# Earlier mark for the first w_up loads, raw pairs in one tile, and w_down's operands in other buffers

## The chip, the cores and the metric

The kernel runs on one core of one Trainium2 chip. The time is the device time of one execution in microseconds (us): a median of runs, and beside it one execution that the hardware profiler took, on which every span and duration below rests. Engines: PE (TensorE), ACT (ScalarE), DVE (VectorE), POOL (GpSimd) and SP (SyncE, which here only issues DMAs). Each engine works through its own instructions in the order of the program; a wait of one instruction holds all that stand behind it on the same engine.

## The reference

Two layers over 512 tokens of 1024 channels, and a last RMSNorm. Of a layer, this is what matters here:

```
mixed = sigmoid(gate_a) * y_a + sigmoid(gate_b) * y_b     # y_b = attention out @ w_o_nsa
x = x + mixed @ w_out                                     # 1024 x 1024
h = rmsnorm(x, norm_mlp)
x = x + square(relu(h @ w_up)) @ w_down                   # 1024 x 4096, 4096 x 1024
```

## The kernel before

**Products.** All is float32. A factor is split in a high part (a cast to fp32r) and a rest, and a product is three matmuls, high x high, high x rest, rest x high. For weights `fetch` (L202) loads a raw block of 512 KB through SP into one of two `raw` buffers, `convert` casts it on ACT (L218, `wh`) and subtracts on DVE (L219, `wl`); `gemm` issues the matmuls, L244 and L245 with `wh` and L246 with `wl`. It converts the next block while one is multiplied. A tile of w_out is 8 steps of three matmuls, 128 x 128 by 128 x 512.

**The end of a layer's attention.** For m = 0..7 the output projection w_o_nsa gives a tile of y_b; L1073 and L1074 (DVE) gate it and add it to MA, four tiles "va" of two halves each: MA[m // 2][:, m % 2]. `mix` (L1055, L1056) halves and splits what is in MA. Then x is loaded, and the loop over w_out's eight tiles runs: `gemm`, L1094 adds the result to x[m], `prepare` scales x[m] and splits it for the MLP (bs L1428, ts L1431, casts L1420 and L1423 on ACT, rests L1421 and L1424 on DVE), `sumsq` squares it on ACT (L288) and adds up on POOL (L298) for the first ones.

**The MLP** is done by a Strassen-like scheme (7 products in place of 8). A unit g takes a pair of w_up's column blocks: `load(g)` loads r2 and r1 (512 KB each, L1476) and s3 (256 KB, L1486) through SP, and POOL issues two DMAs that add within SBUF: r2[:512] += r2[512:] (L1478, the sum s1) and s3 += r1[:512] (L1487). `convert(g)` splits r1 (ACT L1506, DVE L1507), forms a11 = s1 + a11 (DVE L1513), splits r2, forms a12 = a11 + a12 (L1516), splits r1 again and s3. The products of it are the matmuls of L1526. Pairs 0 to 15 are w_up's; 16 to 19 are w_down's last 1024 rows, done the same way in `down` at the MLP's end (L1252 to L1264).

**What sets the order around the change.** The loads of pairs 0 and 1 and the first half of `convert(0)` are issued ahead of and within the w_out loop; unit g loads pair g + 2. To hold the first two pairs' loads back until the attention is over, POOL copies one column of `b.mark` into each of their raw tiles (L1469), and the loads wait for that copy, since they overwrite it:

```
self.mark = MA[3][:, 1, :1]
S.load(0)
S.load(1)
conv = S.convert(0)
```

Buffers are tiles by tag; a tile waits for the last readers of the buffer it takes, and the tiles of the MLP's tags lie over those of the attention. "f" has four buffers of 4 KB a partition (two pairs), "h" two for s3. w_down's Winograd operands b1 and b22 take a "vn", three "q2" and an "hl" tile, and the raw blocks of pairs 18 and 19 the same tags. The scheduler that puts the instructions of each engine in order goes by these buffers, too.

Of the kernel before, what the change touches and what calls it, by code (L numbers as in the profile page):

```python
# [12 lines left out]
F32R = mybir.dt.float32r  # L13
# [130 lines left out]
class Body:  # L144
    def __init__(self, ctx, tc, nc, a):
# [4 lines left out]
        self.ps = P("ps", 2, space=bass.MemoryType.PSUM)  # L150
        self.dp = P("dp", 1, space=bass.MemoryType.DRAM)

    BUFS = dict(raw=2, wh=2, wl=2, u2=8, o2=8, va=4, t2=12, kd=2, kk=1, zz=4, zzm=2, pt=10, long=2, q2=3, vn=1, e=2, cp=2, a4=1, f=4, h=2, a5=2, tmp=3,
                hl=2, r=1, crs=1, zc=4, tt=1, tf=1, small=1, cc=1, s4=6, big=1, g4=2)

    TINY = dict(s4=(4, 12), sm=(4, 8), g4=(4, 2), s16=(16, 2), s32=(32, 5), z=(32, 1), th=(96, 1), gates=(96, 1))
# [1 line left out]
    def t(self, tag, shape, dt=F32, name=None):  # L158
# [8 lines left out]
        if tag in ("tmp", "small") and n < T:  # L167
            v = self.sb.tile([128, T], dt, name=name or tag, tag=tag, bufs=self.BUFS[tag])[:, :n]
            if len(shape) > 2:
# [3 lines left out]
            return v  # L173
        bufs = self.BUFS[tag]
        if tag in self.LOCAL:
            bufs = self.BUFS.get(tag + self.part[0], bufs)
            tag += self.part
# [443 lines left out]
    def compress(self, kc, vc, small, l):  # L621
# [20 lines left out]
        def load(c):  # L642
            for i, raw in enumerate(self.two("o2", "w1", F32) if c < 8 else ()):
                nc.sync.dma_start(raw, a["w1"][l, i, c].rearrange("p j m -> p (j m)"))
                loaded.append(raw)

        load(0)
        load(1)
        for c in range(0, 8, 2):
            load(c + 2)  # L650
            yield
            load(c + 3)
            yield
            w = [loaded.popleft() for _ in range(4)]
            for j in range(4):
                jj = 2 * c + j
                for i in range(2):
                    nc.tensor.matmul(hp[64 * i:64 * i + 64, :256], A[i][jj // 8][:, jj % 8],
                                     w[j // 2 * 2 + i][:, j % 2 * 256:(j % 2 + 1) * 256],
                                     start=jj == 0, stop=jj == 15)  # L660
            yield
            yield
# [97 lines left out]

    BUFS.update(s16=2, sm=8)

# [56 lines left out]

    BUFS.update(th=1, s32=5, gates=1, z=1)  # L820

# [40 lines left out]
    def layer(self, l, u):  # L862
        nc, a = self.nc, self.a
# [3 lines left out]
        va = [self.p(t) for t in ("S", "S", "PT", "PT")]  # L867
# [3 lines left out]
        g = self.token_proj(src, 512, va, u)  # L871
# [7 lines left out]
        g = self.token_proj([[a["wg2"][l, c].rearrange("p j m -> p (j m)")] for c in range(4)], 288, g2, u)  # L879
# [18 lines left out]
        for b in range(NB):  # L898
            pv = g2[b][:, :256].rearrange("p (h d) -> p h d", h=4)
            r = rc[:, b:b + 1]  # L900
# [14 lines left out]
        st, hl = {}, []  # L915
# [59 lines left out]
        MA = [self.t("va", [128, 2, T], name="ma") for _ in range(4)]  # L975
# [83 lines left out]
        for m in range(8):  # L1059
# [12 lines left out]
            t, y = st["gb", m], MA[m // 2][:, m % 2]  # L1072
# [9 lines left out]
            nc.scalar.dma_start(x[k], self.x_src[k])  # L1082
        self.part = f"m{l}"
        S = Strassen(self, l, x, self.gain[:, 16 * l + 8:16 * l + 16])
        self.mark = MA[3][:, 1, :1]
        S.load(0)
        S.load(1)
        conv = S.convert(0)
# [118 lines left out]
class Strassen:  # L1207
# [190 lines left out]
    def prepare(self, m):  # L1398

        b, nc = self.b, self.nc  # L1400
        V, A = nc.vector, nc.scalar
        f = lambda ap: ap.bitcast(F32)
        if m == 0:
            k12 = [b.t("kd", [128, 2, 2, 2, 256], F32R, name="t12") for _ in range(2)]
            k34 = [b.t("long", [128, 2, 2, 2, 256], F32R, name="t34") for _ in range(2)]
            self.k12 = [t[:, i] for t in k12 for i in range(2)]
            self.k34 = [t[:, i] for t in k34 for i in range(2)]
            t = b.t("vn", [128, 2, 2, 2, 256], F32R, name="b1")
            self.k1 = [t[:, 0], t[:, 1]] + [b.t("q2", [128, 2, 2, 256], F32R, name="b1") for _ in range(2)]
            k22 = [b.t(tag, [128, 2, 2, 256], F32R, name="b22") for tag in ("q2", "hl")]  # L1410
            self.k22 = [t[:, i] for t in k22 for i in range(2)]
            t1, t2 = ([t[:, i] for t in self.k12] for i in range(2))
            t3, t4 = ([t[:, i] for t in self.k34] for i in range(2))
            n11, b21 = ([t[:, i] for t in self.k1] for i in range(2))
            self.xs = dict(a11=n11, s1=t1, s2=t2, a22=t4, s3=t3, a12=b21, s4=self.k22)
            self.b1 = {}

        def split(o, x, sign=1.0):
            if sign == 1.0:
                A.copy(o[..., 0, :], x)  # L1420
                V.tensor_tensor(o[..., 1, :], x, f(o[..., 0, :]), op=OP.subtract)  # L1421
            else:
                A.activation(o[..., 0, :], x, AF.Copy, scale=sign)  # L1423
                V.scalar_tensor_tensor(o[..., 1, :], x, sign, f(o[..., 0, :]), op0=OP.mult, op1=OP.subtract)  # L1424

        p = m % 4
        t = b.t("t2", [128, T], name="bs")
        A.activation(t, self.x[m], AF.Copy, scale=self.gm[:, m:m + 1])  # L1428
        if m < 4:
            d = b.t("t2", [128, 2, 256], name="ts")  # L1430
            V.tensor_tensor(d[:, 0], t[:, 256:], t[:, :256], op=OP.subtract)  # L1431
            split(self.k1[p][:, 0], t[:, :256], -1.0)
            split(self.k12[p][:, 0], d[:, 0])
            self.b1[p] = t, d
            return
        t1, d = self.b1.pop(p)
        split(self.k1[p][:, 1], t[:, :256])
        V.tensor_tensor(d[:, 1], t[:, 256:], d[:, 0], op=OP.subtract)
        split(self.k12[p][:, 1], d[:, 1])
        t34 = b.t("t2", [128, 2, 256], name="ts")  # L1440
        V.tensor_tensor(t34[:, 1], t[:, :256], d[:, 1], op=OP.subtract)
        V.tensor_tensor(t34[:, 0], t1[:, 256:], t[:, 256:], op=OP.subtract)
        split(self.k34[p], t34)
        split(self.k22[p], t[:, 256:], -1.0)
# [5 lines left out]
    def load(self, g, third=True):  # L1450

        b = self.b
        if g == 18:
            r = b.t("vn", [128, 2, 1024], name="raw")
            self.rest = [b.t("q2", [128, 2, 512], name="raw") for _ in range(3)]

            for t in [r] + self.rest[1:]:
                self.nc.scalar.copy(t[:, :, :1], self.c[3][:, :, :1])
            r2, r1 = r[:, 0], r[:, 1]
            s3 = self.rest[0][:, 0]  # L1460
        elif g == 19:
            r2, r1 = (t.rearrange("p a c -> p (a c)") for t in self.rest[1:])
            s3 = self.rest[0][:, 1]
        else:
            r2, r1 = (b.t("f", [128, 1024], name="raw") for _ in range(2))
            s3 = b.t("h", [128, 512], name="raw")
            if g < 2:
                for t in (r2, r1, s3):
                    self.nc.gpsimd.tensor_copy(t[:, :1], b.mark)  # L1469
        r1, r2, s3 = self.raw[g] = r1[:, :1024], r2[:, :1024], s3[:, :512]  # L1470
        if g > 17:
            self.nc.sync.dma_start(r1, self.source(g, 1))
            self.nc.sync.dma_start(r2, self.source(g, 0))
            return
        for i, t in enumerate((r2, r1)):
            self.nc.sync.dma_start(t, self.source(g, i))  # L1476
            if t is r2:
                self.nc.gpsimd.dma_start(r2[:, :512], r2[:, 512:], accum_op=OP.add)  # L1478
        if third:
            self.third(g)  # L1480
# [162 lines left out]
```

## Time and profile before

| | us |
|---|---|
| median of 3 runs | 1518.62 (1518.27 to 1518.7) |
| the profiled execution | 1516.23 |
| its span, first to last instruction | 1514.2 |
| DVE busy | 1153.2 |
| ACT busy | 809.8 |

The span is what the profile's times count from; 2 us of the profiled execution lie around it. In a view's row the first number is the start or the busy time, in brackets stands how long the engine idled just before and what it waited for; `x` is the number of instructions. Matmuls overlap in the pipeline: their starts tell the pace, not their lengths. PEclk, or the granted clock, is the share of full speed that PE was given. The mean over the span is 0.995.

The stage of the change in layer 0 runs from about 354 us (the second w_o) to about 422 us (end of w_out), in layer 1 from about 1103 to 1171 us.

### The profile page before, as it was taken

Reading aid. Unit: us, or ns where it says so; the run is one execution under the profiler, and the core shown is the slowest. Engines: PE = TensorE matmul, PEld = TensorE weight load, DVE = VectorE, ACT = ScalarE, POOL = GpSimd, SP = SyncE. Lnnn points to the kernel's source line nnn. Section 1 sums busy time; section 2 is a strip of 40 time slices with the busy share of each in tenths; the row PEclk is TensorE's granted clock in tenths of the full one; section 3 lists DMA queues with packets and bytes.
Section 4 is the critical chain, followed back from the end, with each engine's and each line's share of the span. In section 5 each row is a group of like instructions: output and inputs, shape, how many; then the busy total and the mean of one; then the engine's idle time right before and its main releaser. Section 6 shows DMA issues by size and latency. Waiting matters only on the chain.

```text
span 1514.2 us, 23498 instructions
## 1 busy us (share of the span) xinstructions
PE 1492.2 (99%) x8766; PEld 1299.9 (86%) x8766; DVE 1153.2 (76%) x2245; ACT 809.8 (53%) x1536; POOL 121.2 (8%) x161
## 2 busy tenths in 40 slices
PE   9999999999899999999999999999998999999998
PEld 8888888888699998999988788888876999999998
DVE  5678979777787776678847799787679777677795
ACT  6465656554574444455545556555546544445455
POOL 1010000000300000010010000000013100000112
PEclk9999999999999999999999999999999999999999
DMA  7654422124645555564267552221355555455532
GB/s 249 187 166 126 140 70 70 70 71 155 198 129 148 144 138 146 144 165 110 85 205 186 156 130 92 84 72 69 114 163 148 158 149 137 133 143 139 140 99 70
DMA packets 73921, 200.50 MB, mean 132 GB/s; under 512 B 9264, under 2 KB 10672, under 8 KB 73808
## 3 DMA queue, kind: packets, MB, share of 16 engines
q1 hardware_dynamic: 58256, 171.19, 35.9%
q0 software_dynamic: 11520, 20.98, 8.4%
q10 hardware_dynamic: 4032, 6.84, 1.4%
q8 instruction: 69, 1.13, 0.3%
q14 instruction: 44, 0.36, 0.1%
HBM read 150.67 MB, written 4.19 MB: 102 GB/s over the span
## 4 chain that ended last, share of the span: by engine, by line
PE 75%; issue 19%; DVE 3%; DMA 2%; ACT 0%; POOL 0%; POOLq 0%; SPq 0%; DVEq 0%; ACTq 0%
PE ps_S L1526 8%; PE ps_mm L244 7%; PE ps_mm L245 7%; PE ps_mm L246 7%; PE ps_PT L1526 5%; PE ps_O L244 4%; PE ps_O L246 4%; PE ps_mm L1526 4%; PE ps_O L245 4%; PE ps_O L1526 2%; PE ps_mm L1319 2%; PE ps_S L1319 1%; PE ps_O L612 1%; PE ps_PT L586 1%; PE ps_S L561 1%
## 5 line engine op out<-in xcount | busy, mean ns | idle before, releaser
L218 ACT CAST wh<-raw 128x1024 fp32r<-128x1024 f32 (+2 forms) x161 | 164.7, 1024 | 173.4 <-PE ps_mm L245 51.1
L219 DVE TENSOR_TENSOR wl<-raw,wh 128x1024 fp32r<-128x1024 f32 (+2 forms) x161 | 191.7, 1191 | 33.0 <-ACT wh L218 32.3
L1507 DVE TENSOR_TENSOR s<-raw,s 128x1024 fp32r<-128x1024 f32 (+1 forms) x128 | 139.0, 1087 | 81.9 <-ACT s L1506 81.7
L244 PE MATMUL ps_mm<-u,wh 128*128 128x512 f32 x480 | 192.7, 402 | 0.0
L246 PE MATMUL ps_mm<-u,wl 128*128 128x512 f32 x480 | 189.2, 394 | 0.0
L245 PE MATMUL ps_mm<-u,wh 128*128 128x512 f32 x480 | 189.0, 394 | 0.0
L1506 ACT CAST s<-raw 128x1024 fp32r<-128x1024 f32 (+1 forms) x128 | 120.5, 942 | 80.3 <-PE ps_mm L1526 26.2
L246 PE MATMUL ps_O<-o,wl 128*128 128x512 f32 x280 | 110.2, 393 | 5.8 <-DVE wl L219 5.8
L244 PE MATMUL ps_mm<-o,wh 128*128 128x512 f32 x288 | 113.7, 395 | 0.0
L245 PE MATMUL ps_mm<-o,wh 128*128 128x512 f32 x288 | 113.1, 393 | 0.0
L246 PE MATMUL ps_mm<-o,wl 128*128 128x512 f32 x288 | 112.9, 392 | 0.0
L244 PE MATMUL ps_O<-o,wh 128*128 128x512 f32 x280 | 110.2, 393 | 0.4 <-ACT wh L218 0.4
L245 PE MATMUL ps_O<-o,wh 128*128 128x512 f32 x280 | 110.0, 393 | 0.0
L246 PEld LDWEIGHTS ps_mm<-u,wl 128*128 128x128 f32 x480 | 90.2, 188 | 18.9
L244 PEld LDWEIGHTS ps_mm<-u,wh 128*128 128x128 f32 x480 | 90.5, 189 | 17.9 <-DVE E L462 0.8
L245 PEld LDWEIGHTS ps_mm<-u,wh 128*128 128x128 f32 x480 | 90.4, 188 | 15.7 <-issue 0.4
L1526 PEld LDWEIGHTS ps_S<-t,s 128*128 128x128 f32 x768 | 98.7, 189 | 4.7 <-ACT z L1565 0.4
L1526 PE MATMUL ps_S<-t,s 128*128 128x256 f32 x768 | 101.0, 281 | 0.0
L590 ACT CAST pth<-ps_PT 128x384 fp32r<-128x384 f32 (+1 forms) x96 | 49.0, 513 | 64.8 <-PE ps_PT L586 64.7
L1603 ACT ACTIVATE z<-z 128x512 f32<-128x512 f32 x64 | 40.3, 633 | 78.1 <-DVE z L1602 77.9
L548 DVE CUSTOM_DVE_ANT_0 E<-ps_S,ct 128x384 f32<-128x384 f32 (+3 forms) x112 | 57.2, 513 | 31.7 <-PE ps_S L561 30.8
L549 ACT ACTIVATE E<-E,tiny 128x384 f32<-128x384 f32 (+3 forms) x112 | 65.6, 586 | 20.4 <-DVE tiny L548 20.2
(357 smaller groups left out, 3396.9 us busy)
## 6 DMA issues: line engine op xcount, KB each, us to landing
raw<-wb SPq DMA_DIRECT2D x64, 512.0 KB, 3.2
raw<-wup SPq DMA_DIRECT2D x64, 512.0 KB, 4.3
raw<-wd SPq DMA_DIRECT2D x48, 512.0 KB, 3.7
raw<-raw POOLq DMA_DIRECT2D x80, 256.0 KB, 3.7
w<-w SPq DMA_DIRECT2D x32, 256.0 KB, 4.6
kda<-hla SPq DMA_DIRECT2D x32, 256.0 KB, 4.3
q2a<-hla SPq DMA_DIRECT2D x64, 128.0 KB, 2.3
raw<-wo SPq DMA_DIRECT2D x16, 512.0 KB, 4.4
```

The source lines that it names most:

```text
L218: nc.scalar.copy(h[:, :n], raw[:, :n])
L219: nc.vector.tensor_tensor(lo[:, :n], raw[:, :n], h[:, :n].bitcast(F32), op=OP.subtract)
L244: mm(ps, h[:, c], xh, start=start and i == 0, stop=False)
L245: mm(ps, h[:, c], xl, start=False, stop=False)
L246: mm(ps, lo[:, c], xh, start=False, stop=stop and i == ks - 1)
L548: nc.vector.tensor_tensor_reduce(e, ps, self.mask[:, T - n:], -1.0, BIG, OP.add, OP.min, mx)
L549: nc.scalar.activation(e, e, AF.Exp, bias=mx, scale=-1.0, accum_out=un["sm"][:, i:i + 1])
L590: nc.scalar.copy(h[:, e, :n], ps[:, :n])
L1319: mm = lambda o, *z, **kw: nc.tensor.matmul(o, *z, skip_group_check=True, **kw)
L1506: nc.scalar.copy(h, src)
L1507: nc.vector.tensor_tensor(lo, src, h.bitcast(F32), op=OP.subtract)
L1526: mm = lambda o, *z, **kw: self.nc.tensor.matmul(o, *z, skip_group_check=True, **kw)
```

## The change

The mark becomes MA[0]'s second half, which is the gate's second tile. A pair's r2 and r1 are one tile of 8 KB, with two such buffers in place of four of 4 KB; b1, b22 and the raw blocks of pairs 18 and 19 take "vn" buffers, of which the MLP has three. Behind these lines the new program is four lines shorter, so L1469 is now L1465, L1476 L1472, L1486 L1482, L1506 and L1507 L1502 and L1503, L1513 L1509, L1516 L1512. All of the attention's and MLP's tiles get new addresses: the first two pair tiles now lie side by side at the low end of SBUF, over the attention's keys (tag "kk").

```diff
-... q2=3, vn=1, e=2, cp=2, a4=1, f=4, h=2 ...
+... q2=3, vn=1, vnm=3, e=2, cp=2, a4=1, f=2, h=2 ...
...
-        self.mark = MA[3][:, 1, :1]
+        self.mark = MA[0][:, 1, :1]
...
-            t = b.t("vn", [128, 2, 2, 2, 256], F32R, name="b1")
-            self.k1 = [t[:, 0], t[:, 1]] + [b.t("q2", [128, 2, 2, 256], F32R, name="b1") for _ in range(2)]
-            k22 = [b.t(tag, [128, 2, 2, 256], F32R, name="b22") for tag in ("q2", "hl")]
-            self.k22 = [t[:, i] for t in k22 for i in range(2)]
+            k1 = [b.t("vn", [128, 2, 2, 2, 256], F32R, name="b1") for _ in range(2)]
+            self.k1 = [t[:, i] for t in k1 for i in range(2)]
+            t = b.t("vn", [128, 4, 2, 256], F32R, name="b22")
+            self.k22 = [t[:, i] for i in range(4)]
...
-        if g == 18:
+        if g > 17:
             r = b.t("vn", [128, 2, 1024], name="raw")
-            self.rest = [b.t("q2", [128, 2, 512], name="raw") for _ in range(3)]
-
-            for t in [r] + self.rest[1:]:
-                self.nc.scalar.copy(t[:, :, :1], self.c[3][:, :, :1])
-            r2, r1 = r[:, 0], r[:, 1]
-            s3 = self.rest[0][:, 0]
-        elif g == 19:
-            r2, r1 = (t.rearrange("p a c -> p (a c)") for t in self.rest[1:])
-            s3 = self.rest[0][:, 1]
+            self.nc.scalar.copy(r[:, :, :1], self.c[3][:, :, :1])
+            if g == 18:
+                self.third18 = b.t("vn", [128, 2, 512], name="raw")
+            r2, r1, s3 = r[:, 0], r[:, 1], self.third18[:, g - 18]
         else:
-            r2, r1 = (b.t("f", [128, 1024], name="raw") for _ in range(2))
+            t = b.t("f", [128, 2, 1024], name="raw")
+            r2, r1 = t[:, 0], t[:, 1]
             s3 = b.t("h", [128, 512], name="raw")
```

On SP, behind the four loads of the second w_o in either layer, the difference of the two programs is this (wup are the pairs' loads, r2, r1 and the 512 wide s3; a line with + is the new program's):

```order
+L1472 DMA raw<-wup 128x1024
+L202 DMA raw<-wout 128x1024
+L1472 DMA raw<-wup 128x1024
+L1482 DMA raw<-wup 128x512
+L202 DMA raw<-wout 128x1024
+L1472 DMA raw<-wup 128x1024 x2
+L1482 DMA raw<-wup 128x512
 L202 DMA raw<-wout 128x1024 x3
-L1476 DMA raw<-wup 128x1024 x2
-L1486 DMA raw<-wup 128x512
-L202 DMA raw<-wout 128x1024 x2
```

Pair 0's first load stands ahead of w_out's first, its two others behind that; pair 1's stand behind w_out's second load. Before, all of them stood behind w_out's third.

On DVE, in the w_out loop from x of m = 1 (ps_S is the second tile's bank) the order before is this, with the three rows ahead of it (s is a split of a raw block, 1024 wide for r1 or r2 and 512 for s3; wl in the last row but one is that of m = 3):

```order
L1507 TENSOR_TENSOR s<-raw,s 128x1024
L1421 TENSOR_TENSOR t_3742<-ts,t_3742 128x256
L1507 TENSOR_TENSOR s<-raw,s 128x1024
L1513 TENSOR_TENSOR raw<-raw 128x512
L1094 TENSOR_TENSOR x<-x,ps_S 128x512
L1516 TENSOR_TENSOR raw<-raw 128x512
L1507 TENSOR_TENSOR s<-raw,s 128x512
L1431 TENSOR_TENSOR ts<-bs 128x256
L219 TENSOR_TENSOR wl<-raw,wh 128x1024
L1507 TENSOR_TENSOR s<-raw,s 128x1024
```

And this it is in the new program, to the row behind wl of m = 4:

```order
L1503 TENSOR_TENSOR s<-raw,s 128x1024
L1421 TENSOR_TENSOR t_3740<-ts,t_3740 128x256
L1509 TENSOR_TENSOR raw<-raw 128x512
L1503 TENSOR_TENSOR s<-raw,s 128x512
L1503 TENSOR_TENSOR s<-raw,s 128x1024
L1094 TENSOR_TENSOR x<-x,ps_S 128x512
L1512 TENSOR_TENSOR raw<-raw 128x512
L219 TENSOR_TENSOR wl<-raw,wh 128x1024
L1431 TENSOR_TENSOR ts<-bs 128x256
L1503 TENSOR_TENSOR s<-raw,s 128x1024
L1424 SCALAR_TENSOR_TENSOR b_3744<-bs,b_3744 128x256
L1421 TENSOR_TENSOR t_3740<-ts,t_3740 128x256
```

The splits of s3 and r2 stand ahead of x of m = 1, and wl of m = 3 one row earlier, ahead of ts; behind the last row shown come x of m = 2, one more split (of pair 1's first block), ts, b and then wl of m = 4, which before stood right behind x of m = 2.

On POOL, at the end of layer 0's MLP, the DMAs that add within SBUF stood before in this order (the two pairs are 16 and 17; L1478 is r2's, L1487 s3's, L1264 belongs to `down`):

```order
L1478 DMA raw_6653<-raw_6653 128x512
L1487 DMA raw_6655<-raw_6654 128x512
L1478 DMA raw_6661<-raw_6661 128x512
L1487 DMA raw_6663<-raw_6662 128x512
L1264 DMA raw_6654<-raw_6654 128x512
L1264 DMA raw_6662<-raw_6662 128x512
```

Now they stand so:

```order
L1483 DMA raw_6636<-raw_6635 128x512
L1474 DMA raw_6635<-raw_6635 128x512
L1483 DMA raw_6643<-raw_6642 128x512
L1474 DMA raw_6642<-raw_6642 128x512
L1264 DMA raw_6635<-raw_6635 128x512
L1264 DMA raw_6642<-raw_6642 128x512
```

In either pair s3's sum is now ahead of r2's.

More of the change, by code (lines that the diff above doesn't have):

```diff
@@ L151, in __init__ @@
         self.dp = P("dp", 1, space=bass.MemoryType.DRAM)
-    BUFS = dict(raw=2, wh=2, wl=2, u2=8, o2=8, va=4, t2=12, kd=2, kk=1, zz=4, zzm=2, pt=10, long=2, q2=3, vn=1, e=2, cp=2, a4=1, f=4, h=2, a5=2, tmp=3,
+    BUFS = dict(raw=2, wh=2, wl=2, u2=8, o2=8, va=4, t2=12, kd=2, kk=1, zz=4, zzm=2, pt=10, long=2, q2=3, vn=1, vnm=3, e=2, cp=2, a4=1, f=2, h=2, a5=2, tmp=3,
                 hl=2, r=1, crs=1, zc=4, tt=1, tf=1, small=1, cc=1, s4=6, big=1, g4=2)
```

## The prediction

> **What bounds the kernel now.** I read the page first (busy time, clock row), then PE's waits, then the timeline of the two stretches where the waits lie, then the chain of waits through one of them.
>
> ```profile
> PE 1492.2 (99%) x8766; PEld 1299.9 (86%) x8766; DVE 1153.2 (76%) x2245; ACT 809.8 (53%) x1536; POOL 121.2 (8%) x161
> ...
> PE ps_O L246 <- DVE wl L219: 5.8, 1, 5.8
> PE ps_S L246 <- DVE wl L219: 5.2, 1, 5.2
> PE ps_S L368 <- ACT wh L218: 1.2, 1, 1.2
> ...
> PE ps_S L244 <- ACT wh L218: 0.5, 1, 0.5
> PE ps_O L244 <- ACT wh L218: 0.4, 1, 0.4
> ```
>
> PE is busy 1492.2 of 1514.2 us, so only 22 us of waiting can be had at all, and half of it is two single waits for a `wl`: 5.8 and 5.2 us, one for each layer. The next is 1.2 us. The timeline of PE puts the first at 386 us and the second at 1135 us, both in w_out's fourth tile (m = 3):
>
> ```profile
> 384.98 0.39 PE L246 MATMUL ps_PT<-o,wl 128*128 128x512 f32 x1
> ...
> 386.11 0.40 PE L245 MATMUL ps_O<-o,wh 128*128 128x512 f32 x1
> 392.28 0.80 PE L246 MATMUL ps_O<-o,wl 128*128 128x512 f32 x1 [5.77 <-DVE wl L219]
> ...
> 396.67 0.45 PE L244 MATMUL ps_O<-o,wh 128*128 128x512 f32 x1
> 396.96 0.40 PE L245 MATMUL ps_O<-o,wh 128*128 128x512 f32 x1
> ...
> 1133.91 0.39 PE L246 MATMUL ps_mm<-o,wl 128*128 128x512 f32 x1
> ...
> 1140.74 0.80 PE L246 MATMUL ps_S<-o,wl 128*128 128x512 f32 x1 [5.22 <-DVE wl L219]
> ...
> 1144.58 0.39 PE L244 MATMUL ps_S<-o,wh 128*128 128x512 f32 x1
> ...
> 366.00:386.50 20.50, 20.09 (x88) 16.00 (x86) 12.79 (x19) 10.22 (x18) 4.45 (x8) 1.00 0.72 224
> 392.50:397.00 4.50, 4.48 (x11) 3.04 (x12) 4.50 (x6) 3.04 (x5) 2.82 (x2) 0.53 1.09 291
> ```
>
> The windows show the second half of the price: after the wait the granted clock is 0.53 and PE starts 11 matmuls in 4.5 us; ahead of it the clock is 1.00 and each takes 0.23 us (20.09 / 88). So the loss is best counted by starts. From 384.98 to 396.96, 11.98 us, 13 matmuls start; at 0.2275 us they need 2.96, so **9.0 us** are lost. In layer 1, from 1133.91 to 1144.58, 10.67 us, nine of these start and two half as wide; they need 2.3, so **8.4 us** are lost. Together 17.4 us: all that a change at this place can bring.
>
> Why `wl` is late, by the chain of waits:
>
> ```profile
> 373.53 5.83 DMA raw<-wup
> ...
> 379.93 8.24 DMA raw<-raw
> 388.26 0.69 DVE raw L1513
> 388.95 0.60 DVE x L1094
> 389.55 0.60 DVE raw L1516
> 390.15 0.60 DVE s L1507
> 390.75 0.33 DVE ts L1431
> 391.09 1.15 DVE wl L219
> ```
>
> DVE works in program order. Its L1513 needs the first pair's sum s1, which lies behind POOL's copies of the mark, a load of 5.8 us and an accumulating DMA of 8.2 us; `wl` of m = 3 stands five instructions behind it. No engine was short of time: DVE waited. The start of this chain is the mark:
>
> ```profile
> 354.86 1.28 DVE L1074 TENSOR_TENSOR ma<-ma,gate 128x512 f32<-128x512 f32 x2
> 370.44 0.68 DVE L1074 TENSOR_TENSOR ma<-ma,gate 128x512 f32<-128x512 f32 x1
> ...
> 371.28 2.58 POOL L1469 COPY raw<-ma 128x1 f32<-128x1 f32 x6 [265.57 <-DVE ma L1074]
> ...
> 357.31 9.24 SPq L202 DMA_DIRECT2D raw<-wout  x3
> ...
> 363.46 1.06 ACT L218 CAST wh<-raw 128x1024 fp32r<-128x1024 f32 x1 [2.51 <-PE ps_mm L245]
> ```
>
> **The change part by part.** *The mark.* MA[3]'s second half is final at 371.12 (370.44 + 0.68), MA[0]'s at 356.14 (354.86 + 1.28): the six copies can go 15.0 us earlier, POOL having nothing else (it had waited 265 us). Copying from about 356.3, the first load goes out about 356.8 (it now stands ahead of w_out's first load, which went at 357.3 and so loses nothing), the other two of pair 0 by 358.4, those of pair 1 behind w_out's second load, about 362. With the slowest legs of the chain, 5.83 and 8.24 us, and 0.87 us of POOL between them, pair 0's last sum lands at 358.4 + 5.8 + 0.9 + 8.2 = 373.3; DVE now reaches the first of the sums at 379.1 (below). The DMA wait disappears with almost 6 us to spare.
>
> What is late next? I go down DVE's new row with before's start-to-start times.
>
> ```profile
> 378.39 1.23 DVE L1507 TENSOR_TENSOR s<-raw,s 128x1024 fp32r<-128x1024 f32 x1 [1.06 <-ACT s L1506]
> ...
> 377.31 1.05 ACT L1506 CAST s<-raw 128x1024 fp32r<-128x1024 f32 x1 [0.80 <-DMA raw<-wup]
> ```
>
> ACT's first split waited 0.80 us for the load; without that DVE's begins at 377.6. Then 1.14 (this split), 0.34 (t; a small one as ts in the chain), 0.60 (the sum), 0.60 (s3's split) and 1.14 (r2's split) bring it to 381.4; x 0.60 and the second sum 0.60 to 382.6; `wl` for m = 3 runs from 382.6 to 383.8. PE's last matmul of m = 2 starts at 384.98, so m = 3 begins at 385.2 and its third matmul, the first with `wl`, is due at 385.7: **1.9 us to spare**, where it came 6 us late. Then ts, a split, b, t (0.34 + 1.14 + 0.34 + 0.34) to 386.0, x 386.6, the new second split 387.7, ts and b 388.4: `wl` for m = 4 is done at 389.6, needed a tile later (24 x 0.2275 = 5.46 us), at 391.2: **1.6 us to spare**. From there the row is as before. `wh` for m = 3 is cast on ACT behind two splits, by about 381, long before 385.2, so the 0.4 goes too. Layer 1 has the same rows. Sum of this part: 17.4 us, less what these two margins don't cover: I take 0.4 us a layer.
>
> Where those margins could go, by rows:
>
> ```profile
> 393.28 1.50 DVE L1424 SCALAR_TENSOR_TENSOR b<-bs,b 128x256 fp32r<-128x256 f32 x1
> 397.11 0.41 DVE L1424 SCALAR_TENSOR_TENSOR b<-bs,b 128x256 fp32r<-128x256 f32 x1
> ...
> 392.52 1.98 POOL L298 TENSOR_TENSOR acc<-sq 128x512 f32<-128x512 f32 x1 [1.83 <-ACT sq L288]
> ```
>
> Beside POOL's sum of squares a DVE instruction of 0.41 us took 1.50. That sum runs after each x; with x of m = 1 at 382 it now falls on `wl` of m = 3, or what is next to it. One such hold is 1.1 us: less than either margin; two on one path would cost 0.6 us. The Trainium skill's page "SBUF — State Buffer" (section "Who interferes with whom") says a DVE instruction with two SBUF inputs contends with a GpSimd instruction that reads SBUF, for a pair of ports locked by whoever comes first; the two rows agree. By that rule POOL's six copies would hold up w_o's `wl` too; in before they lie beside a `wl` of the usual length, so the sum stays as it is either way.
>
> *The pair as one tile.* A pair's r2 load now waits until the whole tile is free, not its half.
>
> ```profile
> 549.43 5.91 SPq L1476 DMA_DIRECT2D raw<-wup  x2
> ...
> 553.79 0.86 POOL L1478 DMA_DIRECT2D raw<-raw  x1 [11.32 <-DMA raw<-wup]
> ...
> 581.82 1.05 ACT L1506 CAST s<-raw 128x1024 fp32r<-128x1024 f32 x1 [0.25 <-PE ps_PT L1526]
> ```
>
> In the MLP these two loads went at 549.43 and 555.0; now both go at 555.0, the r1 load when it did. The accumulate moves from 553.8 to about 559.4 and lands by 568 with the slowest leg; the pair's first split is at 581.8. Some 14 us remain: cost nothing, and 1 us at most for the tighter bunch. If that cover were gone, each of 14 units would pay. At the MLP's end the load for pair 17 goes 11 us later:
>
> ```profile
> 678.61 11.45 SPq L1476 DMA_DIRECT2D raw<-wdn  x2
> ...
> 694.50 0.86 POOL L1487 DMA_DIRECT2D raw<-raw  x1 [8.85 <-DVE z L1579]
> ...
> 702.21 1.28 DVE L1252 TENSOR_TENSOR raw<-raw 128x512 f32<-128x512 f32 x2
> ```
>
> It now goes at 689.7; its accumulate stands behind the one of 694.5, at 695.4, and lands 5.8 to 8.2 us later, 701 to 704, where DVE reads it at 702.2 to 703.5. DVE may wait up to 1.5 us; PE's work behind that is several tiles long, so I price it at 0, with 1 us a layer as its other end.
>
> *The rest.* Two ACT copies in place of three for pairs 18 and 19, and w_down's operands in "vn" tiles: no matmul, split or byte changes. New addresses can order some loads of the attention differently; without a row for that I bound it by the smaller PE waits of the list, from -1.2 to +1.2 us, and take 0.
>
> Sum: 17.4 - 0.8 = 16.6 us off the profiled execution's 1516.23, so 1499.6 there. The median of the runs is 1518.62, 2.4 us higher; the same 16.6 us off it give **1502.0**.
>
> **The rivals.** *(a) The margins don't hold.* ACT, POOL and three DMA queues now run closer together, and 1.6 us is two DVE instructions. If one `wl` is 1.5 to 3 us late in each layer, 17.4 falls to between 14.4 and 11.4: 1504 to 1507. For: the 1.50 us row. Against: nothing in the row needs a DMA at that time. The Trainium skill's "TensorE: Matmul & The Clock Gate" (section "Part 1: The HAM clock gate") puts the half rate after an idle window of about 3.4 us; the 0.53 behind the 5.8 us wait agrees. By it waits of 1.5 to 3 us would cost themselves alone; with before's slow stretch behind them (2 us) it would be 1508 to 1511.
>
> *(b) One layer keeps its stall,* for instance since pair 1's loads and w_out's share the DMA engines (share 0.72 in 366 to 386.5, 1.09 in 392.5 to 397) and a sum of pair 1 is late for the row between the two `wl`. It is 8.4 to 9.0 us: about 1510.
>
> *(c) The change doesn't do what it says:* the copies still wait until about 371, for the old owner of the new tiles' place. The same chain, the same 17 us lost: 1518.6. Against it: the tiles lie over the attention's, done before w_o starts.
>
> *(d) Slower.* The first pair load stands ahead of w_out's first load on SP. Were the copies as late as now, that load would go at 372, not 357.3 (when its cast at 363.46 still had to wait for PE, not for it), and land with the chain's 5.8 us by 378. PE begins w_out three tiles ahead of 385.2, at 368.8: up to 10 us of idling and 2 us of slow clock a layer in place of 9.0 and 8.4, so 1518.6 + 24 - 17.4 = 1525. It decides when the first copy is later than about 361: load, cast and split need up to 5.8 + 1.05 + 1.15 = 8.0, and 368.8 less 8.0 is 360.8.
>
> **How the numbers follow.** Forecast (0 to 1 us left in a layer, 1500.5 to 1503.5): 0.64. (a): 0.17. (b): 0.06. (c): 0.05. (d): 0.04. Faster still, by something the new addresses bring: 0.04. The likeliest gives 1502.0. The range of 8 in 10 goes from 1499.5 to 1509: the forecast with a part of the faster case, and (a) with what the slow clock adds to its shorter waits. A measurement of this kernel can tell about 0.2%, 3 us, from no change. Faster: the forecast, (a), (b) and the last, 0.91. Same: (c), 0.05. Slower: (d), 0.04.
>
> **What would show it.** Right: POOL's copies start near 356.3 and SP's first pair load before 358; DVE's first sum waits for no DMA; the two waits for `wl` of over 5 us are gone from PE's list and the clock stays at 1.00 from 366 to 403; PE's busy time falls by about 4 us (slow matmuls) and its idling by 12. Wrong: a wait of over 1 us for `wl` in w_out, copies later than 361, w_out's first cast waiting for its load, or DVE waiting for raw<-raw inside the MLP.

## The result and the profile after

| | before | after |
|---|---|---|
| median, us | 1518.44 (1515.83 to 1518.7, 4 runs) | 1501.45 (1500.94 to 1502.0, 4 runs) |
| profiled execution, us | 1516.23 | 1500.94 |
| its span, us | 1514.2 | 1498.9 |
| PE busy / not busy within the span, us | 1492.2 / 22.0 | 1489.9 / 9.0 |

The changed kernel is faster: ratio 0.9892, 95% interval 0.9875 to 0.9909. 1502.0 was predicted.

The page's first lines, the waits of PE, and windows over the stage in layer 0 (columns as in the prediction):

```profile
span 1498.9 us, 23433 instructions
...
PE 1489.9 (99%) x8766; PEld 1299.4 (87%) x8766; DVE 1149.6 (77%) x2245; ACT 805.7 (54%) x1534; POOL 117.9 (8%) x161
...
PE ps_PT L1192 <- DVE ones L1189: 1.1, 1, 1.1
PE ps_S L368 <- ACT wh L218: 0.7, 1, 0.7
PE ps_PT L586 <- DVE E L573: 0.3, 1, 0.3
...
366.00:386.50 20.50, 20.50 (x91) 16.71 (x90) 18.87 (x30) 14.98 (x26) 3.48 (x3) 1.00 0.80 213
386.50:392.50 6.00, 6.00 (x28) 4.90 (x27) 5.96 (x8) 3.40 (x6) 3.00 (x4) 1.00 0.60 197
392.50:397.00 4.50, 4.50 (x22) 3.64 (x20) 4.25 (x7) 2.46 (x5) 2.09 (x2) 1.00 1.01 219
```

Both waits for `wl` in w_out are gone and nothing has come in their place: PE is busy from 366 to 397 us at a clock of 1.00. From 392.5 to 397 it starts 22 matmuls, where the kernel before started 11. What PE still waits for lies elsewhere, none of it longer than 1.1 us.

### The profile page after: what moved, and what is told of

The parts are those of the page before. It is cut to its first block, busy times and chain, and to the rows that moved or that the text cites. A ratio compares the mean times of both kernels' runs of the same rounds, so it can differ in the third digit from the quotient of the medians.

```text
span 1498.9 us, 23433 instructions
## 1 busy us (share of the span) xinstructions
PE 1489.9 (99%) x8766; PEld 1299.4 (87%) x8766; DVE 1149.6 (77%) x2245; ACT 805.7 (54%) x1534; POOL 117.9 (8%) x161
## 4 chain that ended last, share of the span: by engine, by line
PE 93%; DVE 3%; DMA 1%; issue 1%; ACT 1%; POOL 0%; POOLq 0%; SPq 0%; DVEq 0%; ACTq 0%
PE ps_mm L244 12%; PE ps_mm L245 11%; PE ps_mm L246 11%; PE ps_S L1522 8%; PE ps_PT L1522 5%; PE ps_O L244 4%; PE ps_O L245 4%; PE ps_O L246 4%; PE ps_mm L1522 4%; PE ps_O L612 2%; PE ps_PT L586 2%; PE ps_S L561 2%; PE ps_O L1522 2%; PE ps_mm L1319 1%; PE ps_S L1319 1%; PE ps_PT L472 1%
## 5 line engine op out<-in xcount | busy, mean ns | idle before, releaser
L218 ACT CAST wh<-raw 128x1024 fp32r<-128x1024 f32 (+2 forms) x161 | 164.5, 1024 | 151.8 <-PE ps_mm L245 48.8
L1503 DVE TENSOR_TENSOR s<-raw,s 128x1024 fp32r<-128x1024 f32 (+1 forms) x128 | 139.7, 1095 | 55.7 <-ACT s L1502 55.3
L1502 ACT CAST s<-raw 128x1024 fp32r<-128x1024 f32 (+1 forms) x128 | 120.0, 940 | 31.7 <-PE ps_mm L1522 13.6
```

Of the source, the lines that this page charges most:

```text
L218: nc.scalar.copy(h[:, :n], raw[:, :n])
L1502: nc.scalar.copy(h, src)
L1503: nc.vector.tensor_tensor(lo, src, h.bitcast(F32), op=OP.subtract)
```

## The experiments

The line numbers of each kernel are its own; they differ by up to four. The runs of the kernel before that stood beside the first four experiments have a median of 1519.60 us, beside the next four 1518.72 and beside the last three 1518.99. Single runs of it lie between 1515.28 and 1521.75 us, and the time goes with the clock: 1515.28 to 1517.2 at a mean granted clock of 0.995 or 0.996, 1518.85 to 1520.43 at 0.991.

### The mark alone

In the kernel before, nothing else changed:

```diff
-        self.mark = MA[3][:, 1, :1]
+        self.mark = MA[0][:, 1, :1]
```

> Only the mark moves to MA[0]'s second half; tiles and buffers as in the kernel before. Theory (the mark is all of the gain): POOL's copies start near 356, the two waits for wl of 5.8 and 5.2 us in w_out are gone, the time falls by 15 to 18 us, to 1500.5 to 1503.5. Rival (the new tiles are needed as well, since a first pair's raw tile of before lies over something that is in use until the end of the second w_o): the copies, or some of them, still start at about 365 to 371, at least one stall a layer of 3 us or more stays, and the time is 1508 to 1518.

Measured: 1500.17 us (1499.16 to 1500.64), ratio 0.9874 (0.9861 to 0.9888); a second time, in a later set of runs, 1499.85 us, ratio 0.9877 (0.9861 to 0.9894). The first time is 19.4 us less than that of the kernel before beside it, somewhat more than the 15 to 18 expected, and 0.3 us under the expected range. PE's longest wait is now 1.1 us, and its list has none for `wl`. The mark is all of the gain. Its copies in the timeline of POOL, where the column before the line is the engine:

```profile
356.54 1.96 POOL L1469 COPY raw<-ma 128x1 f32<-128x1 f32 x6 [250.71 <-DVE ma L1074]
```

They wait for the mark and for no former owner of the tiles, so the 4 KB tiles of before would have done.

### The mark and the pair in one tile

As above, and in `load`, with f=2:

```diff
-            r2, r1 = (b.t("f", [128, 1024], name="raw") for _ in range(2))
+            t = b.t("f", [128, 2, 1024], name="raw")
+            r2, r1 = t[:, 0], t[:, 1]
```

> The mark on MA[0] and a pair as one 8 KB tile, with w_down's operands and last raw blocks in the buffers of before. Theory (a pair in one tile costs nothing, since its later r2 load is used over 20 us later): the time of the kernel with the mark alone, within 1.5 us, and no wait for raw<-raw on DVE within the MLP. Rival (the tighter bunch of loads costs in each unit): 3 us or more over the mark alone.

Measured: 1500.80 us (1499.48 to 1502.55), ratio 0.9880 (0.9867 to 0.9893): 0.6 us over the mark alone, and DVE waits for no raw<-raw in the MLP. The ranges of the two overlap, so the later r2 loads cost nothing that can be measured. The `wl` of m = 4 comes a little late in this trace:

```profile
PE ps_mm L246 <- DVE wl L219: 0.4, 1, 0.4
```

### The changed kernel again

> The changed kernel again, beside the others on one chip: 1501 to 1502.5 by its earlier runs. Theory: equal to the mark alone within 1.5 us; rival: the new tiles bring some us of their own, and it is 3 us or more faster than the mark alone.

Measured: 1501.12 us (1500.75 to 1501.49), ratio 0.9881 (0.9868 to 0.9895). That is 0.95 us above the mark alone, within the 1.5 us expected; the section on why shows where most of it lies.

### The operands' buffers alone

The changed kernel with MA[3] as the mark and with four tiles of 4 KB for the pairs; what is left of the change are the buffers of w_down's operands and last raw blocks, of which these lines are a part:

```diff
-            t = b.t("vn", [128, 2, 2, 2, 256], F32R, name="b1")
-            self.k1 = [t[:, 0], t[:, 1]] + [b.t("q2", [128, 2, 2, 256], F32R, name="b1") for _ in range(2)]
+            k1 = [b.t("vn", [128, 2, 2, 2, 256], F32R, name="b1") for _ in range(2)]
+            self.k1 = [t[:, i] for t in k1 for i in range(2)]
```

> Only the vn buffers for w_down's operands and the last raw blocks; mark on MA[3] and four 4 KB tiles as before. Theory: the time of the kernel before within 2 us, with both stalls of over 5 us for wl in w_out. Rival (the operands' buffers shorten the MLP's end or take a wait from it): faster than before by 3 us or more.

Measured: 1520.72 us (1519.99 to 1522.56, 11 runs), ratio 1.0013 (1.0004 to 1.0022). Its PE waits:

```profile
PE ps_PT L244 <- ACT wh L218: 7.8, 1, 7.8
PE ps_O L246 <- DVE wl L219: 5.8, 1, 5.8
```

One stall a layer stays. In layer 1 it is a wait for `wh` and not, as expected, for `wl`, and it is longer. The time is within the 2 us expected: the buffers alone gain nothing and may cost 1 us.

### One split computed again, and again

To see how much room was left at `wl` of m = 4, and what a wait there costs, that split alone was computed two, three and four times in each layer (in `convert`; the results are the same). The lines for two:

```diff
-        nc.vector.tensor_tensor(lo[:, :n], raw[:, :n], h[:, :n].bitcast(F32), op=OP.subtract)
+        for _ in range(2 if str(src) in self.again else 1):
+            nc.vector.tensor_tensor(lo[:, :n], raw[:, :n], h[:, :n].bitcast(F32), op=OP.subtract)
```

> The changed kernel with wl of w_out's fifth tile (m = 4) computed twice in each layer; the second stands behind one small split, so wl is ready 0.33 + 1.22 us after 391.05, at 392.6, and PE's first matmul with it, at 391.48 so far, waits about 1.2 us a layer. Theory (the margin of this wl is nearly used up, 0.4 us, and a short wait costs only itself, with the clock at 1.00): 2.2 to 2.6 us over the changed kernel, about 1503.5. Rival (the margin is the 1.6 us that the prediction worked out): no wait, 1501 to 1502.

Measured: 1504.33 us (1503.56 to 1504.7), ratio 0.9907 (0.989 to 0.9923). The waits of PE:

```profile
PE ps_PT L248 <- DVE wl L221: 1.3, 1, 1.3
PE ps_mm L248 <- DVE wl L221: 1.1, 1, 1.1
```

1.1 us in layer 0 and 1.3 in layer 1, as expected, with the clock at 1.00 behind them; 2.9 us over the 1501.45 of the changed kernel, 0.3 more than expected. The room was some 0.4 us and not 1.6.

> The same with three computations; a sum (0.6 us) and a subtraction (1.14) more stand ahead of the last, so wl is ready at about 394.3 and PE waits about 2.9 us a layer. If waits under 3 us leave the clock alone: 5.8 us over the changed kernel, 1507. If such a wait is followed by the slow clock as the 5.8 us wait was (2 us a layer): 1511.

Measured: 1509.17 us (1507.98 to 1510.24), ratio 0.9938 (0.9923 to 0.9953), between the two expectations. The run does not tell them apart: the scheduler answered with another order on PE, with matmuls of m = 5 and of the MLP ahead of the late ones, so the waits for `wl` are only 1.0 and 1.3 us. The clock is 1.00. Against the changed kernel's trace, whose span is 7.4 us shorter, PE idles 4.3 us more (13.3 us in place of 9.0) and is busy 3.1 us longer (1493.0 in place of 1489.9); what makes it busy longer was not found.

> The same with four: ready at about 396.1, a wait of 4.6 us a layer. With the clock at 1.00: 9.3 us over the changed kernel, 1510.5; with a slow stretch of 2 us behind each wait: 1514.5; with one in one layer only: 1512.5.

Measured: 1511.41 us (1510.83 to 1515.91), ratio 0.9959 (0.9943 to 0.9975). PE's order is another here, too, so the sum of 4.6 us a layer can't be tested. But layer 1 shows one wait by itself (timeline of PE, and a window behind it):

```profile
1144.61 0.79 PE L248 MATMUL ps_PT<-o,wl 128*128 128x512 f32 x1 [2.79 <-DVE wl L221]
1145.20 0.63 PE L246 MATMUL ps_PT<-o,wh 128*128 128x512 f32 x1
1145.62 0.63 PE L247 MATMUL ps_PT<-o,wh 128*128 128x512 f32 x1
...
1145.00:1152.00 7.00, 7.00 (x21) 5.43 (x21) 2.30 (x4) 0.43 (x2) 3.15 (x1) 0.61 0.53 150
```

PE waited 2.79 us, and its matmuls start 0.43 us apart behind that, where 0.23 is usual; the clock is 0.61 in the mean of 7 us. In layer 0 a still shorter wait, for ACT, has the same behind it:

```profile
398.28 0.39 PE L1525 MATMUL ps_S<-b,s 128*128 128x256 f32 x1 [2.35 <-ACT b L1426]
...
399.83 0.63 PE L247 MATMUL ps_mm<-o,wh 128*128 128x512 f32 x1
400.26 0.63 PE L248 MATMUL ps_mm<-o,wl 128*128 128x512 f32 x1
```

So a wait of under 3 us can bring the slow clock. That it always does is not shown: the execution profiled here took 1515.91 us, the other three 1510.83 to 1511.68, and of those there is no trace.

### The mark on MA[2]

The kernel before with a mark in between:

```diff
-        self.mark = MA[3][:, 1, :1]
+        self.mark = MA[2][:, 1, :1]
```

> The tiles of before and the mark on MA[2]'s second half, final at 365.05, 8.9 us later than MA[0]'s and 6.1 earlier than MA[3]'s. By the chain of the kernel before, 6.1 us earlier, the first pair's last sum lands at 382.1, or earlier with the 7.4 us leg of layer 1; DVE's new order needs it at 379.1 to 379.7, so it waits up to 3 us, less 1.9 us of margin at wl of m = 3 and 0.4 at that of m = 4. Theory (that chain alone decides): waits of 0 to 2.5 us a layer, the clock at 1.00, 1500.5 to 1506. Rival (earlier loads help in proportion, or the stall stays until the mark is at MA[0]): 1508 or more, with waits of 3 us or more for wl.

Measured: 1511.56 us (1510.55 to 1514.22), ratio 0.9956 (0.9942 to 0.9971). The theory as stated falls. The time is the rival's, but its waits are not: none for `wl` reaches 3 us. Timelines of DVE, ACT and PE, the chain of waits, and a window:

```profile
384.31 0.69 DVE L1513 TENSOR_TENSOR raw<-raw 128x512 f32<-128x512 f32 x1 [5.30 <-DMA raw<-raw]
...
384.22 1.57 ACT L1506 CAST s<-raw 128x512 fp32r<-128x512 f32 x2 [5.89 <-DMA raw<-raw]
385.70 1.04 ACT L218 CAST wh<-raw 128x1024 fp32r<-128x1024 f32 x1
...
374.54 9.58 DMA raw<-raw
...
386.79 0.50 PE L244 MATMUL ps_O<-o,wh 128*128 128x512 f32 x1 [1.45 <-ACT wh L218]
387.13 0.40 PE L245 MATMUL ps_O<-o,wh 128*128 128x512 f32 x1
389.44 0.50 PE L246 MATMUL ps_O<-o,wl 128*128 128x512 f32 x1 [1.91 <-DVE wl L219]
...
386.50:397.00 10.50, 8.30 (x28) 6.43 (x29) 10.50 (x15) 7.87 (x14) 2.71 (x3) 0.84 0.71 184
```

The chain was the right one, its size was not: the accumulate took 9.58 us from POOL's issue on, not 8.24, and DVE could go on at 384.3, only 4 us earlier than before for a mark 6 us earlier. `wh` of m = 3 is also late, since ACT's new order has s3's split ahead of it. PE waits 1.45 and 1.91 us with two matmuls between, and the slow clock follows again (mean 0.84); layer 1 has the same with 1.73 and 1.91 us. With MA[3], MA[2] and MA[0] as marks the times are 1518.7, 1511.6 and 1500: the gain grows with the time by which the mark is final earlier. The first 6 us bring 7, the next 9 bring 11 to 12, near to proportion, and with MA[0] no wait is left to take away.

### The sums of squares on DVE

In the w_out loop of the changed kernel, and of the mark alone:

```diff
-            acc = self.sumsq(x[m], acc, m > 5)
+            acc = self.sumsq(x[m], acc, True)
```

> The changed kernel with the sums of squares in the w_out loop on DVE in place of POOL. If POOL's sum is what stretched wl of m = 4 from 1.22 to 2.31 us: that row is 1.2 us again, its margin is over 1 us in place of 0.4, and the time stays at 1501 to 1502 (no wait was left to take away). If DVE's longer row (five more of 0.6 us) costs more than the holds: 2 us or more slower, with waits for wl in w_out.

> The mark alone (tiles of before) with the sums on DVE: as the mark alone, 1499.5 to 1501, with wl of m = 4 at 1.2 us. Rival as for the run before: 2 us or more slower.

> The mark alone once more, beside the others: 1499.5 to 1500.7. With the matmuls of w_out at 0.2267 us start to start (0.2302 in the changed kernel) it should be about 1 us faster than the changed kernel; if that difference was chance, within 0.3 us of it.

Measured: with the change 1501.82 us (1500.66 to 1502.74), ratio 0.9890 (0.9875 to 0.9905); with the mark alone 1499.11 us (1498.83 to 1499.62), ratio 0.9873 (0.9857 to 0.9889); the mark alone without it 1499.85 us. `wl` of m = 4 in DVE's timeline of the first and of the second:

```profile
389.36 1.22 DVE L219 TENSOR_TENSOR wl<-raw,wh 128x1024 fp32r<-128x1024 f32 x1
...
386.71 1.22 DVE L219 TENSOR_TENSOR wl<-raw,wh 128x1024 fp32r<-128x1024 f32 x1
```

It takes 1.22 us again, as expected (its place in the row is another, so the margins of these runs and of the earlier ones can't be compared). The changed kernel's time doesn't change by more than its spread, as no wait was left. The mark alone with the sums on DVE is the fastest median of all, 0.4 us under its expected range and 2.7 us below the changed kernel with the same sums; against the mark alone its 0.7 us is within the spread. The mark alone is once more faster than the changed kernel: its nine runs took 1498.73 to 1500.64 us, the eight of the changed kernel 1500.75 to 1502.0. So that difference of about 1 us is hardly chance.

## Why the prediction was right

*The mark.* The timelines of POOL, SP, DVE and PE after:

```profile
356.23 1.97 POOL L1465 COPY raw<-ma 128x1 f32<-128x1 f32 x6 [250.77 <-DVE ma L1074]
...
357.14 0.33 SPq L1472 DMA_DIRECT2D raw<-wup  x1
357.57 0.37 SPq L202 DMA_DIRECT2D raw<-wout  x1
...
379.08 0.69 DVE L1509 TENSOR_TENSOR raw<-raw 128x512 f32<-128x512 f32 x1
...
382.62 1.22 DVE L219 TENSOR_TENSOR wl<-raw,wh 128x1024 fp32r<-128x1024 f32 x1
...
386.50 1.73 DVE L1503 TENSOR_TENSOR s<-raw,s 128x1024 fp32r<-128x1024 f32 x1
...
388.81 2.31 DVE L219 TENSOR_TENSOR wl<-raw,wh 128x1024 fp32r<-128x1024 f32 x1
...
384.76 2.38 POOL L298 TENSOR_TENSOR acc<-sq 128x512 f32<-128x512 f32 x1 [11.47 <-ACT sq L288]
388.61 1.43 POOL L298 TENSOR_TENSOR acc<-sq,acc 128x512 f32<-128x512 f32 x1 [1.47 <-ACT sq L288]
...
391.48 0.39 PE L246 MATMUL ps_mm<-o,wl 128*128 128x512 f32 x1
```

Copies from 356.2 (356.3 was predicted), the first load at 357.1, w_out's own at 357.6, pair 0's last sum landed at 374.1 (373.3 was predicted; issued at 364.64, it took 9.5 us), the first sum on DVE at 379.1 without a wait, `wl` of m = 3 from 382.6 to 383.8 as worked out. Shown by the mark alone: this is the whole gain.

One link of the chain before was misread, without a change to the sum. The accumulating DMA of 8.24 us, issued at 379.93, is not s1's but s3's (before):

```profile
375.95 1.00 POOL L1478 DMA_DIRECT2D raw<-raw  x1 [2.09 <-DMA raw<-wup]
379.93 0.87 POOL L1487 DMA_DIRECT2D raw<-raw  x1 [2.98 <-DMA raw<-wup]
...
383.63 1.05 ACT L1506 CAST s<-raw 128x1024 fp32r<-128x1024 f32 x1 [4.36 <-issue]
...
388.25 0.62 ACT L1506 CAST s<-raw 128x512 fp32r<-128x512 f32 x1 [2.53 <-DMA raw<-raw]
```

ACT could split r2, with s1 in it, at 383.63. L1513 began at 388.26, when s3's split could begin, too: it overwrites r1[:512], which s3's DMA still read. What had to come earlier was s3's load and sum; the prediction's 373.3 is for this last sum, so its figure holds.

*The margin at m = 4.* It was predicted at 1.6 us, to lose 1.1 to one hold by POOL and to cost 0.6 if two fell on the path. The first hold was expected at `wl` of m = 3; but POOL's first sum began only at 384.76, and two fell on the path of m = 4: the split at 386.50 took 1.73 us beside POOL's first sum, and `wl` 2.31 beside the second. It ended at 391.12, and PE used it at 391.48: 0.36 us to spare, so no cost, by little: the second hold was 1.1 us and the first only 0.5, and PE came 0.3 us later than worked out. The split is 1.22 us again with the sums on DVE, so POOL was the cause; the split computed twice shows that the room was this small. The predicted 0.4 us of residue a layer did not come in the changed kernel, which was luck in part: with the mark and the pair in one tile PE waited 0.4 us here.

*The addresses.* They were taken at 0. From one tile of w_out in layer 0 to the next PE needs, in the changed kernel and then with the mark alone (same order on PE, 24 matmuls a tile, tiles of before):

```profile
385.49 0.40 PE L244 MATMUL ps_O<-o,wh 128*128 128x512 f32 x1
...
391.01 0.40 PE L244 MATMUL ps_mm<-o,wh 128*128 128x512 f32 x1
...
385.33 0.39 PE L244 MATMUL ps_O<-o,wh 128*128 128x512 f32 x1
...
390.77 0.39 PE L244 MATMUL ps_mm<-o,wh 128*128 128x512 f32 x1
```

5.52 us against 5.44, 0.2300 against 0.2267 a matmul. Over eight tiles that is 0.64 us; in layer 1 the tiles take 5.50 and 5.48 us. In layer 0 the slower pace came only with all of the change: with the mark and the pair in one tile, and with the operands' buffers alone, it is 5.44 us. That the addresses decide is likely, but no run moved them alone.

The starts of the same matmuls, counted from the first, tell where the gain lies. From the 1,500th (287 us) to the 2,500th (468 us) and from the 6,000th (1056 us) to the 7,000th (1233 us), stretches with one stage each, both traces of the changed kernel gain 8.1 and 8.2 us on the kernel before, and both traces of the mark alone 8.4 to 8.5 and 8.6. So the mark brought 17.0 to 17.1 of the 17.4 us counted, and the changed kernel's tiles and buffers lost 0.8 to 0.9 us of that, a part of it by the slower pace. The 0.8 us taken off for residue had about the right size, but stood for something else: that is luck. PE's busy time fell by 2.3 us and not by 4, its idling by 13.0 (12 predicted); with the mark alone the busy time fell by 3.1 to 3.2, so the tiles are a part of what is missing there.

*The pair in one tile.* The SP and POOL rows of the same unit, and the end of the MLP; by layer 0's gain PE is 8.3 us earlier at the first rows and 7.8 at the last:

```profile
546.67 0.80 SPq L1472 DMA_DIRECT2D raw<-wup  x2
...
551.07 0.86 POOL L1474 DMA_DIRECT2D raw<-raw  x1 [16.51 <-DVE s L1503]
...
680.77 0.80 SPq L1472 DMA_DIRECT2D raw<-wdn  x2
...
694.29 1.28 DVE L1252 TENSOR_TENSOR raw<-raw 128x512 f32<-128x512 f32 x2
```

Less 8.3 us, the predicted 555.0 for the loads and 559.4 for the accumulate are 546.7 and 551.1, as measured. At the MLP's end the load was predicted at 689.7, less 7.8 is 681.9, and went 1.1 us earlier than that; its reader on DVE waits for nothing. The price of 0 is shown by the pair in one tile beside the mark alone.

*The rivals.* (a) did not happen, but its room was 0.4 us. Of its two prices the lower one, without a slow clock, can't be relied on: the waits of 2.79 and 2.35 us, and of 1.45 and 1.91 close together, were followed by the slow clock; those of 1.0 to 1.3 were not. The Trainium skill's rule (its page "TensorE: Matmul & The Clock Gate", section "Part 1: The HAM clock gate") asks for an idle window of 3.4 us, and by it waits of 1.5 to 3 us cost themselves alone; the traces do not agree with that. The price of a slow stretch was low, too: 2 us were taken, where the prediction's own count leaves 2.8 (9.0 less the waits of 5.77 and 0.41) and 2.7 us (8.4 less 5.22 and 0.48). (b) and (c) did not happen. (d), late copies with the pair's load ahead of w_out's on SP, was not tried.

*The gain itself* is 17.0 us by medians and 15.3 by the two profiled executions, for 16.6 predicted: the profiled execution of before was 2.2 us under its median, so the sum made against it, 1499.6, is 1.3 us below the 1500.94 measured. Of the 15.3, the two stretches gave 16.2; behind the 7,000th matmul the changed kernel was 1.1 us slower, and the mark alone as well (0.9 and 1.1), so the change's other parts are not the cause; what is was not found. The price was read from one of the faster executions of before, with a clock of 0.995. With the later runs beside it the gain is 18.5 us for the changed kernel and 19.1 to 19.4 for the mark alone, more than the 17.4 that the prediction called all there was: in most executions the slow clock of before seems to cost more. So the mechanism was right and its price held for the profiled execution; that the median came within 0.6 us of 1502.0 is luck in part.

## What to carry to other kernels

Where an engine that works in order waits for a DMA, find the first event that lets the chain begin, and ask whether it could be an earlier one of the same kind: here one index of the mark was worth 1.2%, and the tiles around it nothing. When such a wait goes, go down the new order row by row with the measured durations to the next margin, and count the rows that get longer beside another engine's work, as DVE's did beside POOL's sums: they took most of the second margin. Read a price from more than one execution where the clock differs between them. A stall of PE can cost a slow clock as well, even when it is shorter than 3 us.

## What the runs showed of the hardware

- The slow clock (starts 0.43 us apart in place of 0.23) after waits of PE of 2.35 and 2.79 us, and of 1.45 and 1.91 us with about 0.6 us of matmuls between them. Single waits of 1.0 to 1.3 us left the clock at 1.00.
- The same matmuls in the same order start 0.2267 us apart in w_out of layer 0 in the kernel before, with the mark alone, with the mark and the pair, and with the operands' buffers alone, and 0.2300 in both traces of the changed kernel. What decides was not found.
- A DVE split of 1.22 us takes 1.73 to 2.31 us beside a POOL sum of 128x512; without POOL's sums it takes 1.22.
